# Which queue issues the conditioning loads of a hybrid decoder layer: GpSimd's or SyncE's, from the output gate's stage on

## The chip, the cores and the metric

The kernel runs on one NeuronCore of a Trainium2 chip. That core has five engines with instruction streams of their own: TensorE (PE, matrix products), VectorE (DVE), ScalarE (ACT), GpSimd (POOL) and SyncE (SP, which computes nothing and issues transfers). Sixteen DMA engines move data between main memory and the on-chip memory. A transfer is issued by an instruction in the stream of SP, ACT or POOL; in the profile the transfers of SP stand as queue q1, those of POOL as q0, and those of ACT as q10. An engine works through its instructions in order, so an instruction that waits for a semaphore holds up everything behind it on that engine.

The metric is the device time of one launch in microseconds. The kernel before takes 1963.89 us (median of 3 runs, 1963.37 to 1964.3).

## What is computed

One inference step of one layer (`DEPTH = 1`), in float32, for 256 prompt tokens and 8 x 4 sample tokens together: N = 288 columns, model width 2048.

```python
mod = silu(c) @ w_ada + b_ada                       # 2048 -> 6 x 2048
sh1, sc1, gt1, sh2, sc2, gt2 = split(mod, 6)
xn = rmsnorm(x, g_norm1) * (1 + sc1) + sh1
proj = xn @ w_in
...
merged = (gate0 * (y_lru @ w_br_lru) + gate1 * (y_gla @ w_br_gla)
          + gate2 * (y_ml @ w_br_ml))               # y_ml = sigmoid(m_o) * rmsnorm(h)
x = x + gt1 * (merged @ w_out)
xn = rmsnorm(x, g_norm2) * (1 + sc2) + sh2
x = x + gt2 * (square(relu(xn @ w_ff1)) @ w_ff2)
y = rmsnorm(x, g_final)
```

The conditioning product is the first line: `w_ada` is a 2048 x 12288 matrix (six pieces of 2048 columns), multiplied by only nine vectors (one for the prompt, eight for the samples). Its results are needed at different times: sc1 and sh1 at the start, gt1 when the output projection ends, sh2 and sc2 for the second norm, gt2 at the very end. The three recurrent branches (RG-LRU, GLA, mLSTM) also read and update states; the one that matters here is the mLSTM's matrix memory of the samples (`state_mlstm_C`, read as 16 tiles `mC`, written as `o_C_s`).

## The kernel before

**The weight stream.** All large products go through `stream` (line 148). It walks a weight block in groups of 256 rows x 512 columns (one tile of 128 x 1024, 512 KB). For each group SP loads `raw` (line 155), ACT makes the rounded `hi` (line 156), DVE makes the rest `lo` (line 158), and PE runs 24 matmuls (line 165: four column blocks, two row blocks, and the products hi x xh, hi x xl, lo x xh). `raw`, `hi` and `lo` have three buffers each. `run` (line 191) drives a stream: after each group it takes one step of the pattern in `pace` and one step of each generator in `side` (the recurrent branches, which run between the groups).

**The conditioning product.** `units` (line 344) yields its pieces: 64 units of 1 MB for GT1, SH2, SC2 and GT2 (16 each), after the smaller ones for SC1 and SH1. A unit has a load (`ada`, line 302; the transfer is line 308, or line 306 twice where the tile is in two halves) and a product (`products`, matmuls on line 269). `load_one` (line 356) issues the next unit's load, `visit` (line 361) runs the products of all units held. A pattern set by `every` is a string of steps, one for each group: `L` loads one unit, `V` visits, `.` does nothing; `skip` leaves out that many groups first. `slots["ids"]` says which buffers the units take in turn: `None` is the tile `ag`, `"st"` the two tiles `st`, a number one of the ten slots `s0` to `s9`, `"xh"` and `"xl"` halves of the tiles that held the activations. `slots["queue"]` says which engine issues the load.

**The queues.** SP's order is written out by hand: `manual_schedule` (line 68) keeps its instructions in the order in which the program emits them. The orders of the other engines come from a planner that places instructions by priority and expected time, so that POOL may issue a load well before the place where the program emits it. The first conditioning loads go through SP (line 235); line 588, ahead of the stage of the remaining value columns, sets the queue to POOL, and nothing sets it again. POOL issues the `mC` loads of the mLSTM too (line 1396); ACT issues its stores (line 1437).

**The stages around the change**, in program order:

- `merge(1)` (line 1512) ends; its last gate tile is in `ag` (line 1085), its last activations are in slots 8 and 3.
- The output gate's stage, lines 1513 to 1523: two blocks of eight groups. Units go to `ag` and slot 8. The pattern loads after the 12th and the 13th of the 16 groups and visits after the 15th. The mLSTM runs beside it: every three groups a pair of `mC` tiles is used (`inter`, line 1412), updated and stored, in two `st` tiles or two halves of slot 9 by turns.
- `merge(2)`, from line 1524: 48 groups, units in `ag`, `st`, slot 5. From the seventh group on, in rounds of seven: three loads after three successive groups, a visit after the next, then three groups without a step. Six rounds, 18 units.
- The output projection, from line 1530: 32 groups. Loads after groups 7 to 12 (six in succession), a visit after the 14th, then eight more loads after groups 16, 17, 19, 20, 22, 23, 25, 26, which are visited at the end of the stage, beside the second norm. 14 units.
- The feed-forward part, from line 1633: the last six units, after groups 1, 4 and 7 of rounds of 20 groups with the visit after the 13th, from the second hidden block on.

That is 2 + 18 + 14 + 6 = 40 units from line 1513 on. Ten of them go to `st` and take two transfers, so there are 50 transfers.

Of the kernel before, what the change touches and what calls it, by code (L numbers as in the profile page):

```python
# [52 lines left out]
def trunk(ctx, tc, io):  # L53
    nc = tc.nc
    PSUM = bass.MemoryType.PSUM
    V, S, G, T, Q = nc.vector, nc.scalar, nc.gpsimd, nc.tensor, nc.sync
# [130 lines left out]
    def every(p, skip=0):  # L187

        pace.update(every=p.split(), n=-skip)
# [45 lines left out]
    slots = {"ids": (None,), "n": 1, "queue": Q}  # L235
# [1274 lines left out]
    ml_ = beside(mlstm())  # L1510

    merge(1, ygla, io["wbg"])
    slots.update(ids=(None, 8), n=0)
    every("L L . V" + 12 * " .", skip=11)

    mo = slot(3)
# [255 lines left out]
```

## Time and profile before

| what | before |
|---|---|
| median of 3 runs | 1963.89 us |
| profiled execution, its own time | 1962.52 us |
| its span, first to last instruction | 1960.7 us |
| PE busy | 1921.1 us (98%) |
| DVE / ACT / POOL busy | 1028.6 / 823.7 / 267.2 us |
| main memory read / written | 409.85 / 16.81 MB |
| mean granted TensorE clock | 0.995 |

The profiled execution's time is 1.8 us above its span: what lies ahead of the first and behind the last instruction. The median of the runs is 1.37 us above the profiled execution. Times inside the trace count from the span's start. A name such as `st<-wada` is a transfer into the tile `st` from the tensor `wada`; `PE pi L1412` is a matmul on line 1412 that writes the tile `pi`. A row of the view of waits tells who waited for whom, the total, how many times and the longest. A row of the view by stretch gives the busy time of PE, weight loads, DVE, ACT and POOL with their numbers of instructions, then the granted clock, the DMA engines' busy share and GB/s.

### The profile page before, as it was taken

To read this page: it belongs to the slowest core of one execution; us is meant where nothing else is said; L and a number is where in the kernel's file an instruction comes from. 1 tells how busy PE (TensorE), PEld (TensorE's weight loads), DVE (VectorE), ACT (ScalarE), POOL (GpSimd) and SP (SyncE) were. 2 spreads that over 40 slices of the span, in tenths; PEclk is the share of its full clock that TensorE was granted. 3 is DMA by queue.
4 is the path that set the end of the run, shared out by engine and by line. 5 is a ranking of instruction groups with operands and counts; after the bars stand their busy time and mean duration, and the time that the engine had idled before them with its cause. 6 is when DMAs were issued, how large, how long until landed. Compare 5 with 4: busy or idle time off the path is not lost.

```text
span 1960.7 us, 35959 instructions
## 1 busy us (share of the span) xinstructions
PE 1921.1 (98%) x15060; PEld 1819.7 (93%) x15060; DVE 1028.6 (52%) x1567; ACT 823.7 (42%) x1179; POOL 267.2 (14%) x373
## 2 busy tenths in 40 slices
PE   7999999999999998999999999999999999999997
PEld 4889889999899997899998899999999999999997
DVE  2574746545683456654445564445444445444565
ACT  3433374544454343443333453443333334343433
POOL 0011200000132000012224431000000000010101
PEclk9999999999999999999999999999999999999999
DMA  9998766547744368957797555444444444444442
GB/s 385 408 381 301 262 243 239 199 151 262 267 149 145 136 205 296 310 215 272 276 360 280 190 187 204 169 159 169 169 163 160 172 162 162 162 168 170 164 172 106
DMA packets 116338, 429.01 MB, mean 219 GB/s; under 512 B 11776, under 2 KB 12064, under 8 KB 116048
## 3 DMA queue, kind: packets, MB, share of 16 engines
q1 hardware_dynamic: 85888, 313.26, 44.1%
q0 software_dynamic: 25536, 96.27, 13.4%
q10 hardware_dynamic: 4752, 17.19, 2.2%
q8 instruction: 118, 1.93, 0.4%
q14 instruction: 44, 0.36, 0.1%
HBM read 409.85 MB, written 16.81 MB: 218 GB/s over the span
## 4 chain that ended last, share of the span: by engine, by line
PE 93%; DMA 4%; DVE 2%; ACT 1%; issue 0%; DVEq 0%; SPq 0%; ACTq 0%; POOLq 0%
PE mm L165 83%; PE pa L269 4%; DMA raw<-win 2%; DMA st<-mC 1%; DMA raw<-wout 1%; DVE lo L158 1%; DMA s<-wada 0%; ACT hi L156 0%; PE px L677 0%; PE px L1429 0%; PE pi L1412 0%; PE px L948 0%; PE px L1343 0%; DVE s L597 0%; DMA o_C_s<-st 0%
## 5 line engine op out<-in xcount | busy, mean ns | idle before, releaser
L158 DVE TENSOR_TENSOR lo<-raw,hi 128x1024 fp32r<-128x1024 f32 x448 | 552.0, 1233 | 591.6 <-ACT hi L156 577.0
L156 ACT ACTIVATE hi<-raw 128x1024 fp32r<-128x1024 f32 x448 | 473.9, 1060 | 797.2 <-PE mm L165 656.8
L165 PE MATMUL mm<-xh,hi 128*128 128x288 f32 x2560 | 757.1, 300 | 2.9 <-ACT xh L493 1.8
L165 PE MATMUL mm<-xl,hi 128*128 128x288 f32 x2560 | 753.4, 297 | 0.0
L165 PE MATMUL mm<-xh,lo 128*128 128x288 f32 x2560 | 737.3, 296 | 1.6 <-DVE lo L158 1.6
L165 PE MATMUL mm<-s,hi 128*128 128x288 f32 x3328 | 659.5, 296 | 0.8 <-DVE rs_t L1545 0.8
L165 PEld LDWEIGHTS mm<-s,hi 128*128 128x128 f32 x3328 | 529.3, 188 | 6.3 <-issue 5.8
L165 PEld LDWEIGHTS mm<-xh,hi 128*128 128x128 f32 x2560 | 479.8, 188 | 21.8 <-issue 12.3
L165 PEld LDWEIGHTS mm<-xl,hi 128*128 128x128 f32 x2560 | 481.9, 188 | 2.7 <-issue 1.3
L165 PEld LDWEIGHTS mm<-xh,lo 128*128 128x128 f32 x2560 | 476.0, 188 | 4.2 <-DVE lo L158 2.7
L165 PE MATMUL mm<-s,lo 128*128 128x288 f32 x1664 | 477.3, 295 | 0.6 <-DVE lo L158 0.6
L165 PEld LDWEIGHTS mm<-s,lo 128*128 128x128 f32 x1664 | 308.6, 188 | 2.0 <-DVE lo L158 1.0
L158 DVE TENSOR_TENSOR lo<-s,hi 128x1024 fp32r<-128x1024 f32 x80 | 98.0, 1225 | 115.2 <-ACT hi L156 115.2
L1607 POOL TENSOR_TENSOR t<-t 128x288 f32<-128x288 f32 x64 | 60.2, 952 | 625.7 <-ACT t L1606 625.7
L156 ACT ACTIVATE hi<-s 128x1024 fp32r<-128x1024 f32 x80 | 84.9, 1061 | 143.2 <-PE mm L165 142.6
L1623 DVE TENSOR_TENSOR s<-s,mm 128x288 f32<-128x288 f32 x96 | 40.3, 450 | 33.9 <-PE mm L165 32.7
L269 PE MATMUL pa<-s,silc 128*32 128x256 f32 (+1 forms) x616 | 49.8, 450 | 5.5 <-DMA s<-wada 5.5
L269 PEld LDWEIGHTS pa<-s,silc 128*32 128x32 f32 x616 | 18.9, 112 | 25.5 <-issue 11.1
L429 DVE TENSOR_TENSOR s<-t,s 128x288 fp32r<-128x288 f32 x64 | 33.8, 568 | 15.5 <-ACT s L428 15.5
L308 POOL DMA_DIRECT2D ag<-wada x23 | 16.5, 719 | 169.7 <-PE pa L269 169.5
L428 ACT ACTIVATE s<-t 128x288 fp32r<-128x288 f32 x64 | 28.1, 443 | 24.6 <-POOL t L1607 24.6
L395 POOL TENSOR_TENSOR row<-row,t 128x288 f32<-128x288 f32 x24 | 22.4, 934 | 116.1 <-ACT t L393 115.1
(403 smaller groups left out, 1117.8 us busy)
## 6 DMA issues: line engine op xcount, KB each, us to landing
raw<-win SPq DMA_DIRECT2D x192, 512.0 KB, 4.4
raw<-wf SPq DMA_DIRECT2D x176, 512.0 KB, 4.1
s<-wf SPq DMA_DIRECT2D x80, 512.0 KB, 3.2
s<-wada SPq DMA_DIRECT2D x28, 1024.0 KB, 9.2
ag<-wada POOLq DMA_DIRECT2D x23, 1024.0 KB, 7.2
s<-wada POOLq DMA_DIRECT2D x21, 1024.0 KB, 10.9
raw<-wout SPq DMA_DIRECT2D x32, 512.0 KB, 4.7
st<-wada POOLq DMA_DIRECT2D x28, 512.0 KB, 8.0
```

The costliest lines, as they stand in the source:

```text
L156: pace["hi"] = S.activation(hi, raw, AF.Copy)
L158: pace["lo"] = V.tensor_tensor(out=lo, in0=raw, in1=hi.bitcast(F32), op=ALU.subtract)
L165: pace["last"] = T.matmul(ps, w[:, kk, ms], x, start=k == k0 and i == 0, stop=k == kt - 1 and i == 2)
L269: pace["prod"] = T.matmul(ps[32 * j:32 * j + 32, h * w // 4:(h + 1) * w // 4], stat(k), v[:, j], start=k == 0 and h == 0, stop=k == KT - 1 ...
L308: slots["queue"].dma_start(raw[0].rearrange("p (h m) -> p h m", h=2), wada[kind, :, k].rearrange("h p m -> p h m"))
L395: G.tensor_tensor(out=s, in0=s, in1=sq, op=ALU.add)
L428: S.activation(dst_h[:, r], src[:, r], AF.Copy)
L429: V.tensor_tensor(out=dst_l[:, r], in0=src[:, r], in1=dst_h[:, r].bitcast(F32), op=ALU.subtract)
L1607: G.tensor_tensor(out=r, in0=r, in1=r, op=ALU.mult)
L1623: V.tensor_tensor(out=a, in0=a, in1=p, op=ALU.add)
```

## The change

One line: where the output gate's stage sets the buffers of its units, it also sets the queue back to SyncE's. Since nothing sets the queue later, this holds for all 40 units from there to the end. Their loads keep their place in the program, their buffers and their visits. Because SP's order is the program's order, each load now stands on SP between the weight load of the group after which the pattern has its `L` and the weight load of the next group; on POOL they are gone.

```diff
@@ -1510,7 +1510,7 @@
     ml_ = beside(mlstm())
 
     merge(1, ygla, io["wbg"])
-    slots.update(ids=(None, 8), n=0)
+    slots.update(ids=(None, 8), n=0, queue=Q)
     every("L L . V" + 12 * " .", skip=11)
 
     mo = slot(3)
```

## The prediction

> **What bounds the kernel now.** I began with the page's head and its table of queues, then asked for PE's waits in the part of the span that the change touches.
>
> ```profile
> span 1960.7 us, 35959 instructions
> PE 1921.1 (98%) x15060; PEld 1819.7 (93%) x15060; DVE 1028.6 (52%) x1567; ACT 823.7 (42%) x1179; POOL 267.2 (14%) x373
> ...
> q1 hardware_dynamic: 85888, 313.26, 44.1%
> q0 software_dynamic: 25536, 96.27, 13.4%
> ```
>
> PE is busy 98% of the span: a change of queues can only win back idle PE time, or add some. The waits of PE between 755 and 1290 us, from the first moved load to the last visit, are three:
>
> ```profile
> PE pi L1412 <- DMA st<-mC: 7.6, 1, 7.6
> PE mm L165 <- DVE rs_t L1545: 0.8, 1, 0.8
> PE mm L165 <- DVE lo L158: 0.6, 1, 0.6
> ```
>
> The large one is a state tile of the mLSTM that came late. POOL's timeline shows what was issued around it, PE's timeline the gap, and the chain of waits the transfer itself:
>
> ```profile
> 755.39 0.53 POOL L1396 DMA_DIRECT2D st<-mC  x1 [7.83 <-DVE s L1110]
> 755.91 0.71 POOL L308 DMA_DIRECT2D s<-wada  x1
> 756.62 0.72 POOL L308 DMA_DIRECT2D ag<-wada  x1
> 758.37 0.56 POOL L1396 DMA_DIRECT2D st<-mC  x1 [1.03 <-DMA o_C_s<-st]
> ...
> 767.16 0.29 PE L165 MATMUL mm<-xl,hi 128*128 128x288 f32 x1
> 775.07 1.08 PE L1412 MATMUL pi<-st,s 128*32 128x257 f32 x8 [7.62 <-DMA st<-mC]
> ...
> 758.37 16.66 DMA st<-mC
> ```
>
> Two conditioning loads of 1 MB went into POOL's queue at 755.91 and 756.62, and the second `mC` load of the pair, issued behind them, took 16.66 us. These two are exactly the units of the output gate's stage: the planner had issued them as soon as their buffers were free. The transfers issued between 755 and 776 us, by queue (kind, size, median us to landing), show that those in POOL's queue came last:
>
> ```profile
> raw<-win SPq DMA_DIRECT2D x3, 512.0 KB, 10.4
> o_C_s<-s ACTq DMA_DIRECT2D x2, 514.0 KB, 8.8
> ag<-wada POOLq DMA_DIRECT2D x1, 1024.0 KB, 16.8
> ```
>
> By stretch (columns as told above):
>
> ```profile
> 767.00:772.00 5.00, 0.45 (x4) 0.21 (x2) 0.90 (x3) 2.77 (x6) 0.54 (x1) 1.00 1.02 418
> 772.00:775.00 3.00, 0.00 (x0) 0.00 (x0) 0.00 (x0) 0.00 (x0) 0.53 (x1) 0.50 1.03 404
> 775.00:779.00 4.00, 3.93 (x21) 3.12 (x22) 2.44 (x6) 0.00 (x0) 0.00 (x0) 0.52 0.17 68
> 779.00:800.00 21.00, 21.00 (x166) 19.87 (x166) 12.25 (x23) 8.80 (x14) 1.58 (x3) 1.00 0.86 280
> 1006.00:1031.00 25.00, 23.68 (x176) 23.07 (x174) 11.25 (x13) 8.79 (x10) 0.36 (x1) 1.00 0.96 387
> ```
>
> The DMA engines were full during the wait (418 and 404 GB/s), and the idle PE lost its clock: it worked from 775 to 779 us at 0.52. The last row is the other weak place, the start of the output projection, where PE is idle for 25.00 - 23.68 = 1.3 us.
>
> **The change part by part.** *The two loads of the output gate's stage leave POOL's queue.* The `mC` load at 758.37 then has nothing between it and the pair's first. What such loads take otherwise (least, median, most, first those from 690 to 756 us, then from 765 to 806):
>
> ```profile
> DMA to landing us min/median/max: 4.5/6.1/7.7
> DMA to landing us min/median/max: 4.0/6.0/7.7
> ```
>
> At the most, 7.7 us, it lands at 766.1, ahead of PE's arrival at about 767.45 (the start of PE's last matmul, and its length). So I take the whole wait: -7.6 us, with bounds 0 (it lands as late as now) and -7.6. The clock goes with it: (1 - 0.52) x 4 us = -1.9 us, bounds 0 and -1.9. The Trainium skill (TensorE: Matmul & The Clock Gate, "What's actually happening") puts the half clock after one idle window of about 3.4 us; the trace agrees, with 7.6 us idle and 0.50 from 772 on, and by that rule a rest of the wait under 3 us would cost no clock.
>
> *Where the two loads go.* On SP they stand behind the 12th and 13th weight loads of the stage:
>
> ```profile
> 790.50 8.41 SPq L155 DMA_DIRECT2D raw<-win  x3
> ...
> 824.65 1.85 PE pa L269 x16
> ```
>
> These three weight loads are the 12th to 14th (the gate's 16 begin 11 loads earlier, at the end of merge 1's), so the loads move from 756 to some 35 us later, 9.5 us less when PE is ahead by that. Their visit is at 824.65, so they are not late. But there they meet `mC` loads and stores of the next pairs: the stretch from 779 to 800 moved 280 GB/s x 21 us = 5.9 MB, and with 2.1 MB more it is 8.0 MB, 380 GB/s, against 404 to 418 in the full stretches. It fits, barely. I set +0.5 us, with bounds 0 and +5.1 (the 2.1 MB at 415 GB/s, all of it falling on one late `mC` tile).
>
> *What stands behind a 1 MB load on SP.* A weight load is not needed at once. The groups, from the chain of waits, and the makers of `hi` and `lo`, from the page:
>
> ```profile
> 863.68 2.72 PE pa L269 x32
> 866.39 22.58 PE mm L165 x168
> ...
> L158 DVE TENSOR_TENSOR lo<-raw,hi 128x1024 fp32r<-128x1024 f32 x448 | 552.0, 1233 | 591.6 <-ACT hi L156 577.0
> L156 ACT ACTIVATE hi<-raw 128x1024 fp32r<-128x1024 f32 x448 | 473.9, 1060 | 797.2 <-PE mm L165 656.8
> ...
> L155 SPq DMA_DIRECT2D raw<-win x20: 327/328/328, 864.3 to 961.3; - x20
> ...
> DMA to landing us min/median/max: 3.1/4.2/8.2
> ```
>
> 168 matmuls are seven groups, so a group is 3.22 us; ACT waits for PE, not for data, 656.8 us in all. With three buffers each, `raw` of group g can be loaded when `lo` of g-3 is made, that is when PE has ended g-6 plus the split of 1.06 + 1.23 = 2.3 us; PE wants it split when it ends g-1. From issue to need that leaves 5 x 3.22 - 2 x 2.3 = 11.5 us, of which the landing takes 4.2 (the median; 3.1 at least, so 1.9 us beside the 1.26 us that 0.52 MB takes at 415 GB/s).
>
> *Merge 2* is the tightest, since SP must wait there: the load into `ag` stands four groups behind the visit that frees it, and SP runs five to six groups ahead of PE. The visit of 863.68 ends at 866.4; only then does SP issue three units and, between and behind them, three weight loads, 3 x 1.05 + 3 x 0.52 = 4.7 MB. At 415 GB/s the last weight tile lands 11.3 + 1.9 = 13.2 us later; it is needed after six groups less the split, 19.3 - 2.3 = 17.0 us. Margin 3.8 us, cost 0. That SP's queue alone reaches such a rate is in the stretch from 0 to 30 us, slow start included (all queues, then q1 with its packets, MB and share):
>
> ```profile
> DMA packets 3088, 11.45 MB, mean 382 GB/s; under 512 B 223, under 2 KB 351, under 8 KB 3087
> q1 hardware_dynamic: 2719, 9.97, 82.7%
> ```
>
> *The output projection* has six loads in succession: per group 1.57 MB, 3.8 us at 415 GB/s against 3.22, a backlog of 6 x 0.6 = 3.4 us, under the 11.5 - 3.2 = 8.3 us left. Before, eight units were asked for at once there, ahead of the weights, at 387 GB/s; spread out and in order they should give back some of the idle 1.3 us. I take -1.0, bounds -1.3 and +3 (about the backlog, uncovered).
>
> *Issuing.* SP gets 50 issues of 0.328 us, 16 us, covered by its waits for buffers. POOL loses these:
>
> ```profile
> L308 POOL DMA_DIRECT2D s<-wada x13: 703/706/775, 755.9 to 1215.7; - x13
> L308 POOL DMA_DIRECT2D ag<-wada x11: 703/721/772, 756.6 to 1216.5; - x11
> ...
> L306 POOL DMA_DIRECT2D st<-wada x20: 528/544/561, 811.1 to 1217.8; - x20
> ```
>
> With six into `xh` and `xl`, 30 x 0.71 + 20 x 0.54 = 32 us. PE's waits above name no POOL work, so both are 0. In the feed-forward part the loads are three groups apart with visits six groups later: 0.
>
> **Sum:** -7.6 - 1.9 - 1.0 + 0.5 = -10.0 us against the profiled execution's 1962.5 (span 1960.7), so 1952.5; the median of the runs lies 1.4 above it: 1953.9 us.
>
> **The rivals.** *Bytes, not queues.* The stall could come from full DMA engines rather than from the order inside POOL's queue; then it only moves to a later `mC` pair. For it: 404 to 418 GB/s during the wait, and 380 expected after 779. Against it: in the same 20 us the stores took 8.8 and the weights 10.4, the `mC` load 16.66, and the stretch after it needs 380 only if nothing spreads. Price: 5.1 us of wait and most of the clock's and the projection's gain, some 9 us given back: 1963. The Trainium skill (DMA: Bandwidth & Descriptors, "Issuing engines are not separate DMA queues") says that all issuers share the same engines and that only issue time is saved, which alone gives this outcome. Its section "Queues, rings and completion order" has each engine take turns between the queues, which speaks for the order inside one queue; the 16.66 beside 8.8 agrees with that.
>
> *SP's queue starves the weights*, the slower side. Weight loads that had a queue of their own stand behind 1 MB loads and behind SP's wait for `ag`. It decides by the rate SP's queue gets. At 290 GB/s merge 2 needs 16.2 + 1.9 against 17.0, 1.1 us in each of five rounds; the projection's backlog is 6 x 2.2 = 13.2 against 11.5 - 3.7 = 7.8, 5.4 more: 11 us, the gain is gone. At 270 it is 5 x 2.3 + 8 = 19.5 us: 1973. For it: SP does wait, and margins are 3 to 5 us. Against it: the 382 GB/s above.
>
> *Half.* The `mC` load still takes as long as the weights did, 10.4 us, and lands at 768.8, 1.4 us late, and the later pairs lose 3 us more: +4, 1958.
>
> **How the numbers follow.** Forecast 0.68, with its own range from 1951 (all bounds on the good side but for noise) to 1957.5 (3 to 4 us of contention); bytes 0.13; starved 0.13; half 0.06. A measurement of this kernel tells 0.2%, 3.9 us, from no change. Faster: 0.68 + 0.06 = 0.74; same 0.13; slower 0.13. The range from 1950.5 to 1965 takes in the forecast, the half and the first rival, and leaves out most of the starved case.
>
> **What would show it.** Right: in the changed profile PE's wait for `st<-mC` is gone, the clock stays 1.00 near 770 us, `mC` loads land within 8 us or so, and PE works without new waits in merge 2. Wrong: an `mC` wait at a later pair (bytes); waits of PE for `lo` or of ACT for `raw` after each visit of merge 2 or in the projection (starved); or a planner's new order that puts something else in front of PE, which the rows before cannot show.

## The result, and the profile after

| | before | after |
|---|---|---|
| median of the runs | 1963.63 us (4 runs, 1961.43 to 1964.3) | 1949.83 us (4 runs, 1949.48 to 1950.38) |
| ratio after / before | | 0.9932, 95% interval 0.9915 to 0.9949 |
| span of the profiled execution | 1960.7 us | 1947.9 us |
| mean granted clock | 0.995 | 0.998 |

The kernel is 13.8 us faster by the medians, 12.8 us by the spans. The forecast was 1953.9 us with a range from 1950.5: the direction and the main cause were right, the gain was 3.8 us more than the 10.0 of the forecast, and the time is just under the range.

The list of PE's waits between 740 and 1290 us is empty in the changed profile: the three waits shown before are all gone. Where the time went is seen best when the same group's first matmul is looked up in both traces (us from the span's start; the groups are those of the weight stream):

```
group                          before     after     after - before
output gate, 3rd               762.39     762.26     -0.1
output gate, 5th               780.41     770.59     -9.8
merge 2, 1st                   830.44     819.93    -10.5
output projection, 7th        1021.84    1011.17    -10.7
output projection, 13th       1042.94    1030.31    -12.6
stream, end of last matmul     1945.56    1932.89    -12.7
```

Nearly all of it falls in two places: 9.7 us at the late `mC` tile, 2.0 us at the start of the output projection; 0.9 us lie in smaller steps between. POOL's timeline after has no conditioning load among the `mC` loads, and SP's has them between the weights:

```profile
753.97 0.53 POOL L1396 DMA_DIRECT2D st<-mC  x1 [7.32 <-PE mm L165]
758.24 0.53 POOL L1396 DMA_DIRECT2D st<-mC  x1 [3.74 <-DMA o_C_s<-st]
...
779.90 0.33 SPq L155 DMA_DIRECT2D raw<-win  x1
780.58 0.38 SPq L308 DMA_DIRECT2D ag<-wada  x1
785.85 0.33 SPq L155 DMA_DIRECT2D raw<-win  x1
786.28 0.38 SPq L308 DMA_DIRECT2D s<-wada  x1
```

The second `mC` load was issued at 758.24, as before at 758.37, and landed in 6.5 us. All 16 `mC` loads now land within 9.6 us, where one took 16.66 before; the 9.6 is that of the load at 781.26, beside the two conditioning loads on SP, and a little over the 8 us or so that the prediction named as the sign of being right (least, median, most):

```profile
DMA to landing us min/median/max: 3.6/6.1/9.6
```

By stretch, the rows that answer to those shown of before; the last is the stretch of 1006 to 1031 us of before, moved by the 10.6 us that PE is ahead:

```profile
767.00:772.00 5.00, 5.00 (x39) 5.00 (x40) 3.97 (x11) 2.95 (x7) 0.53 (x1) 1.00 0.99 311
772.00:775.00 3.00, 3.00 (x25) 3.00 (x24) 2.59 (x5) 0.64 (x1) 0.00 (x0) 1.00 0.90 304
775.00:779.00 4.00, 4.00 (x39) 3.25 (x38) 1.57 (x2) 3.40 (x7) 0.53 (x1) 1.00 0.98 307
779.00:800.00 21.00, 21.00 (x185) 20.36 (x184) 13.97 (x33) 7.44 (x12) 1.59 (x3) 1.00 0.99 377
995.40:1020.40 25.00, 25.00 (x190) 25.00 (x189) 13.20 (x22) 9.23 (x12) 2.06 (x3) 1.00 0.96 365
```

PE is busy throughout and its clock stays at 1.00. The stretch from 779 to 800 us moves 377 GB/s, against the 380 worked out in the prediction, and no work of PE comes late in it. The last row is where the prediction's arithmetic failed: 190 matmuls in 25 us against 176 before, 14 more at 0.134 us each (22.58 us for 168), which is 1.9 us, although the busy column differs by only 1.3 us. (Both traces hold all 24 matmuls of all 528 groups, so none of the 14 is a missing record.)

### The profile page after: what moved, and what is told of

Its sections match the earlier page's. It is cut to its first block, busy times and chain, and to the rows that moved or that the text cites. A ratio compares the mean times of both kernels' runs of the same rounds, so it can differ in the third digit from the quotient of the medians.

```text
span 1947.9 us, 35935 instructions
## 1 busy us (share of the span) xinstructions
PE 1917.1 (98%) x15060; PEld 1816.6 (93%) x15060; DVE 1030.4 (53%) x1567; ACT 824.0 (42%) x1179; POOL 235.9 (12%) x323
## 4 chain that ended last, share of the span: by engine, by line
PE 96%; DVE 1%; DMA 1%; ACT 1%; issue 0%; DVEq 0%; SPq 0%; ACTq 0%
PE mm L165 85%; PE pa L269 5%; DMA raw<-win 1%; PE px L1429 0%; DMA s<-wada 0%; PE px L677 0%; PE pi L1412 0%; DVE lo L158 0%; ACT hi L156 0%; PE px L948 0%; PE px L1343 0%; DVE s L597 0%; PE px L1353 0%; PE pi L966 0%; PE px L1015 0%
## 5 line engine op out<-in xcount | busy, mean ns | idle before, releaser
L1110 POOL TENSOR_TENSOR s<-s,t 128x288 f32<-128x288 f32 x16 | 20.0, 1274 | 179.0 <-DVE t L1109 179.0
```

What stands on the lines that cost most here:

```text
L1110: (V if br == 1 else G).tensor_tensor(out=a, in0=a, in1=t, op=ALU.add)
```

## The experiments

Each is a whole kernel, run beside the kernel before on the same chip. The kernel before had medians of 1962.89, 1962.77 and 1962.83 us in the three groups of runs, and each ratio is to the kernel before of the same group. Edits are shown against the changed kernel. "By the starts of PE's groups" means the difference between two traces in the start of the same weight group's first matmul.

**Which loads carry the gain: the gate's two alone.**

```diff
-    slots.update(ids=(None, "st", 5), n=0)
+    slots.update(ids=(None, "st", 5), n=0, queue=G)
```

> Only the two loads of the output gate's stage go through SP; the 38 from merge 2 on go through POOL as before. If the gain is the late mC tile and its half clock, 9.7 us of the 12.8 us of the changed profile are here, and the start of the output projection loses its 2.2 us again (start to start of PE's groups): about 1952 us, with no PE wait for st<-mC. If the gain came mainly from the 38 other loads, it stays above 1958.

Measured: 1952.31 us (1951.89 to 1953.2), ratio 0.9947 (0.9932 to 0.9961). No wait for `st<-mC`, clock 1.00. PE's waits in the trace are two at the projection, as before (0.8 and 0.5 us), and one of 0.7 us for an `mC` tile ahead of the output gate's stage. Two of the 40 loads carry 10.6 us.

**The other half: the 38 later loads alone.**

```diff
-    slots.update(ids=(None, 8), n=0, queue=Q)
+    slots.update(ids=(None, 8), n=0)
...
-    slots.update(ids=(None, "st", 5), n=0)
+    slots.update(ids=(None, "st", 5), n=0, queue=Q)
```

> The opposite half: the two loads of the output gate's stage stay on POOL, the 38 others go through SP. Theory of the late mC tile: the wait of about 7.6 us and a stretch of half clock near 772 us are there again, the projection's 2.2 us are won: about 1960.5 us. Rival (the other 38 loads carry the gain): under 1954.

Measured: 1962.08 us (1959.21 to 1963.78), ratio 0.9995 (0.9985 to 1.0004). Of PE's waits from 740 to 1290 us only this is left:

```profile
PE pi L1412 <- DMA st<-mC: 6.1, 1, 6.1
```

The half clock is there for 6.8 us again. The projection's 2.0 us are won in the trace (its 13th group comes 2.0 us earlier against its 7th), but the medians differ by only 0.8 us, and the expected time was 1960.5. The late tile itself is not the same from one execution to the next: in the three profiled ones that have it at this place (before, this kernel and a later one) it lands in 16.66, 15.39 and 15.11 us and PE waits 7.6, 6.1 and 6.7. That this hides the projection's gain in the medians is likely, not shown.

**Order in the queue, or bytes: the same bytes at the same time, through SP.** The two loads stand after the 4th and 5th group; their visit stays.

```diff
-    every("L L . V" + 12 * " .", skip=11)
+    every("L L" + 9 * " ." + " V" + 12 * " .", skip=3)
```

> All 40 loads on SP, but the two of the output gate's stage stand after its 4th and 5th group, so that SP issues them when ag comes free, near 755 us, just when POOL issued them before; their visit stays after the 15th group. The same bytes in the same 20 us, in another queue. If the order inside POOL's queue made the mC tile late: the tile lands within 10 us of its issue, PE waits 1 us at most there, 1950 to 1952 us. If full DMA engines made it late, whatever the queue: mC lands after 14 us or more, PE waits 5 us or more and loses the clock, 1956 to 1960 us.

Measured: 1954.06 us (1953.32 to 1954.53), ratio 0.9956 (0.9939 to 0.9972). SP issues the loads at the time when POOL issued them before:

```profile
754.91 0.38 SPq L308 DMA_DIRECT2D ag<-wada  x1
755.38 0.42 SPq L155 DMA_DIRECT2D raw<-win  x1
755.91 0.43 SPq L308 DMA_DIRECT2D s<-wada  x1
```

The `mC` load issued at 757.48 lands in 10.1 us, not 16.7, the clock stays up, and PE waits 1.6 us for a later `mC` tile. The fair pair for it is the kernel just above, which also has the 38 others on SP and differs by the queue of the two early loads: 1962.08 against 1954.06, 8.0 us. So most of the loss was the order inside POOL's queue. Asking for the loads 25 us earlier still costs 4 us against the changed kernel, 2 more than expected. The chain of waits has a weight load behind the first of them and the later `mC` tile:

```profile
755.38 10.98 DMA raw<-win
...
786.24 9.13 DMA st<-mC
```

How much of the 4 us is full DMA engines, and how much weights that now stand behind 1 MB loads on SP, is not told apart.

**The loads on POOL, held back.** A first attempt asked the planner to put each load behind the `hi` of its group:

```diff
-    slots.update(ids=(None, 8), n=0, queue=Q)
+    slots.update(ids=(None, 8), n=0, queue=G, placed=True)
...
-            held.append((u[0], u[1](), u[2], u[3]))
+            with tc.issue_after(pace["hi"].ins) if slots.get("placed") else nullcontext():
+                held.append((u[0], u[1](), u[2], u[3]))
```

> All 40 loads stay on POOL, but the planner may not put them ahead of the hi of the group after which the program has them, so that they are issued about when SP would. If it is the time of issue (the planner's 35 us ahead of the program) and not the queue that costs: no wait of 5 us or more for mC, 1950 to 1954 us. If POOL's queue is the trouble at any time: an mC tile of a later pair comes late behind the two loads and PE waits again 5 us or more, 1957 to 1964 us.

Measured: 1962.09 us (1959.99 to 1964.32), ratio 0.9994 (0.9985 to 1.0003). It tells nothing of either theory, since the loads did not move: placed behind an instruction of ACT, they still went out on POOL near 755 us (one added line moves 1396 to 1397).

```profile
754.66 0.53 POOL L1397 DMA_DIRECT2D st<-mC  x1 [7.62 <-DVE t L1110]
755.18 0.71 POOL L308 DMA_DIRECT2D s<-wada  x1
755.88 0.72 POOL L308 DMA_DIRECT2D ag<-wada  x1
759.24 0.56 POOL L1397 DMA_DIRECT2D st<-mC  x1 [2.63 <-DMA o_C_s<-st]
```

Placed behind an instruction of POOL itself, they do move. The next two kernels put the gate's two loads on POOL behind a chosen `mC` load, and keep the 38 others on SP (added lines move 1396 to 1400 and 1412 to 1416):

```diff
+    mc_load = {}
...
-            G.dma_start(tiles[n], io["mC"][n])
+            mc_load[n] = G.dma_start(tiles[n], io["mC"][n])
...
-    slots.update(ids=(None, 8), n=0, queue=Q)
+    slots.update(ids=(None, 8), n=0, queue=G, behind=12)
...
-    slots.update(ids=(None, "st", 5), n=0)
+    slots.update(ids=(None, "st", 5), n=0, queue=Q, behind=None)
...
-            held.append((u[0], u[1](), u[2], u[3]))
+            b = slots.get("behind")
+            with tc.issue_after(mc_load[b].ins) if b is not None else nullcontext():
+                held.append((u[0], u[1](), u[2], u[3]))
```

> The two loads of the output gate's stage go through POOL, placed right behind the mC load of tile 12 and so ahead of those of tiles 13, 14 and 15, near 778 us, about when SP issues them in the changed kernel; the other 38 stay on SP. If it is the order inside POOL's queue: the load of tile 13 takes 13 us or more, PE waits 4 to 6 us for it about 795 us, 1954 to 1958 us. If only the time of issue counted (the early issue beside a fuller stage): no new mC wait over 1 us, 1949 to 1951 us as with SP.

Measured: 1958.72 us (1956.35 to 1959.9), ratio 0.998 (0.997 to 0.9989). POOL's timeline, the chain of waits and PE's wait show the old picture two pairs later:

```profile
777.05 0.53 POOL L1400 DMA_DIRECT2D st<-mC  x1 [6.27 <-DVE lo L158]
777.57 0.71 POOL L308 DMA_DIRECT2D ag<-wada  x1
778.27 0.72 POOL L308 DMA_DIRECT2D s<-wada  x1
780.65 0.56 POOL L1400 DMA_DIRECT2D st<-mC  x1 [1.66 <-DMA o_C_s<-st]
...
780.65 16.66 DMA st<-mC
...
PE pi L1416 <- DMA st<-mC: 5.5, 1, 5.5
...
799.00:802.00 3.00, 3.00 (x14) 3.00 (x14) 2.04 (x6) 0.00 (x0) 0.00 (x0) 0.50 0.33 129
```

The load behind the two takes 16.66 us again, PE waits 5.5 us, and then works at 0.50 of its clock. The two loads go out 3 and 8 us earlier than in the changed kernel (777.57 and 778.27 against 780.58 and 786.28), in which the same `mC` load, issued at 781.26, took 9.6 us with them on SP. The time is 0.7 us above the expected range.

> As before on POOL, but behind the last mC load (tile 15), near 797 us; the other 38 on SP. Order inside POOL's queue: nothing stands behind the two loads, so no wait, 1949 to 1951 us: POOL's queue is as good as SP's. If POOL's queue as such were the trouble: 1953 or more.

With `behind=15`: 1951.26 us (1950.24 to 1952.12), ratio 0.9941 (0.9925 to 0.9958). The loads go out on POOL at 795.86 and 796.57, nothing that PE awaits stands behind them, and the largest `mC` wait is 0.4 us. POOL's queue as such is not the trouble. The medians lie 1.4 us above the changed kernel's, and 0.3 above the expected range. The spans differ by 1.7 us: 0.5 us is already there at the gate's first group, 0.3 come between there and merge 2, and 0.9 behind the last weight group. I leave that difference open.

**Whether SP's wait can starve the weights.** The visit of merge 2 stands two groups later, so the next load into `ag` follows it by two groups.

```diff
-    every("L L L V . . .", skip=6)
+    every("L L L . . V .", skip=6)
```

> Changed kernel, but in merge 2 the visit stands two groups later, so that the next load into ag stands two groups behind the visit that frees it instead of four. Theory that SP's wait holds up the weights behind it: by the margin of 3.8 us less two groups of 3.22 us, weights come 2.6 us late in each of five rounds: 8 to 18 us more, 1958 to 1968 us, with waits of PE for lo after each visit. Rival (SP's wait is covered by the three buffers anyway): within 2 us of 1949.8.

Measured: 1961.49 us (1960.09 to 1964.48), ratio 0.9995 (0.9986 to 1.0004), 11.7 us above the changed kernel. SP's waits and PE's, in merge 2:

```profile
SPq L308 <- PE pa L269: 46.8, 5, 11.0
...
PE mm L165 <- ACT hi L156: 7.5, 9, 1.3
```

SP waits for the visit before the load into `ag`, five times, and PE then waits for `hi` (`lo` was expected), made from weights that stood behind. By the starts of PE's groups merge 2 is 13.1 us longer than in the changed kernel: 2.6 on average in each of five rounds, as worked out.

> The same late visit in merge 2, with the loads from merge 2 on through POOL (the gate's two on SP), so that the wait for ag holds up POOL and not the weights. Same theory: about as the kernel with only the gate's two loads on SP, 1951 to 1954 us. Rival (the late visit itself costs, whatever the queue): as much slower as its twin on SP.

The same late visit with the loads on POOL (`queue=G` from merge 2 on): 1952.14 us (1952.1 to 1954.74), ratio 0.995 (0.9935 to 0.9965). PE waits nowhere in merge 2. A late visit costs nothing when the wait for its buffer stands on POOL; 2.2 us are lost at the projection, as in the kernel with only the gate's loads on SP.

**The margin at the projection.** Eight loads behind four groups:

```diff
-    every("L L L L L L . V ." + " L L ." * 4 + 20 * " .", skip=6)
+    every("LL LL LL LL . . . V ." + " L L ." * 3 + 20 * " .", skip=6)
```

> Changed kernel, but the output projection loads eight units behind four groups, two behind each, where it loaded six behind six; the visit after the 14th group stays, six more units follow. Per group 2.62 MB, 6.3 us at 415 GB/s against 3.2: a backlog of four times 3.1 us, against some 4 us that lo is ahead of PE when the loads begin: weights 8 us late, PE waits 6 to 10 us, 1956 to 1960 us. If SP's queue did not starve the weights (margin of 8 us as predicted): 1950 to 1954 us.

Measured: 1964.94 us (1963.12 to 1968.46), ratio 1.0013 (1.0004 to 1.0023). PE's waits and SP's in that stage:

```profile
PE mm L165 <- ACT hi L156: 7.4, 4, 2.8
...
SPq L308 <- PE pa L269: 18.7, 1, 18.7
```

By the starts of PE's groups the burst costs 7.3 us, as expected. Another 6.1 us are lost at a second place that the expectation missed: with eight loads ahead, the next two go into halves of `xh` two groups behind the visit that frees them, and SP waits 18.7 us there with the weights behind it. PE's clock fell to half twice, for 3.4 us each. A further 1.2 us were lost in the gate's stage, which this edit leaves as it is, with a wait of 1.0 us for an `mC` tile.

**All conditioning loads through SP.**

```diff
-    slots.update(ids=(5, 6, 7, None, 0, 3), n=0, queue=G)
+    slots.update(ids=(5, 6, 7, None, 0, 3), n=0)
```

> All conditioning loads through SP: also those from the stage of the remaining value columns up to the gate's stage, 13 + 3 of the shift product and the units of merge 0 and 1 among them. PE waits nowhere in that stretch on POOL's loads, so the theory (only a late tile that PE waits for counts) says no change: 1948.5 to 1951.5 us, unless a load waits on SP for its buffer and holds up weights, which would show as waits of PE for lo between 140 and 740 us. Rival (SP's queue is the better one everywhere): 1947 us or less.

Measured: 1954.97 us (1952.78 to 1956.57), ratio 0.9959 (0.9944 to 0.9974): 5 us worse than the changed kernel. Between 140 and 760 us SP now waits for visits:

```profile
SPq L308 <- PE pa L269: 63.7, 12, 11.7
SPq L320 <- PE pa L269: 21.4, 5, 7.1
...
PE mm L165 <- DVE s L1106: 1.9, 1, 1.9
PE mm L165 <- DVE lo L158: 1.4, 2, 0.7
PE mm L165 <- ACT hi L156: 1.0, 1, 1.0
```

PE's waits there are small singly, but its groups fall behind by 3.5 us between 215 and 252 us, and by 1.0 and 1.6 us near 339 and 492 us. SP's queue is not the better one everywhere. That it is so where the pattern leaves enough groups between a visit and the next load into its buffer fits these waits and those of merge 2, but was not varied in this stretch. None of these kernels beats the changed one.

## Why the prediction was right, and where it failed

**The step that failed** is the sizing of three smaller terms of the sum, not its mechanism. The collision was put at +0.5 us with a bound of 0 on the good side, and -0.7 came; the output projection was put at -1.0 with a bound of -1.3, and -2.0 came; the 1.4 us added for the distance between the median and the profiled execution were 0.1 after the change. With every bound on its good side the sum is 1962.5 - 10.8 = 1951.7 us for the profiled execution; it was 1949.74.

**The late `mC` tile: right.** Forecast -7.6 us of wait and -1.9 us of clock, -9.5; by the starts of PE's groups it is -9.7. That the order inside POOL's queue made it late is shown from three sides: the same bytes at the same time through SP give 10.1 us of landing and no loss of clock; the two loads on POOL ahead of a later tile bring the wait and the half clock back there; behind the last tile they cost no wait. The view of transfers from 755 to 776 us of before has the other of the two loads too, and that from 763 to 771, when all three queues had work, what each queue moved (packets, MB, share):

```profile
s<-wada POOLq DMA_DIRECT2D x1, 1024.0 KB, 11.8
...
q0 software_dynamic: 312, 1.20, 36.7%
q1 hardware_dynamic: 297, 1.09, 33.4%
q10 hardware_dynamic: 279, 1.04, 32.0%
```

POOL's queue landed its transfers in the order of their issue: `s` at 767.7, `ag` at 773.4, `mC` at 775.0. It moved 1.20 MB in 8 us beside the other two queues, so that 2.1 MB take some 14 us (an estimate from these rows), and the tile stood behind them. The rival of bytes has at most a smaller share: loading early through SP costs 4 us.

The Trainium skill (DMA: Bandwidth & Descriptors, "Issuing engines are not separate DMA queues") says that issuing from several engines saves issue time alone. Here the measurement decides against it: 8.0 us lie between the two early loads on SP and on POOL. By the Trainium skill's section "Queues, rings and completion order" on the same page, each engine takes turns between the queues it has work for. The three nearly equal rows agree with that, as do the stores of ACT's queue that landed in 8.4 and 9.3 us beside POOL's 16.66 in the run with the loads ahead of tile 13.

One remark of the prediction on the clock does not hold: that a rest of the wait under 3 us would cost none. In the kernel with the doubled loads waits of 2.51 and 2.78 us were enough (the rows stand in the last section).

**The collision of the two loads at their new place: right in its traffic, wrong in its price.** 377 GB/s came, 380 were worked out, but the +0.5 us was not paid. From the 5th gate group to merge 2 PE gained another 0.7 us; the kernel with only the gate's loads moved has it too, the one with only the 38 others moved has not, so it goes with these two loads. What it is made of stays open: the planner also put PE's own instructions in another order there, which no run separates.

**The output projection: a bound that was none.** The prediction took -1.0 us with a bound of -1.3, because the idle time of the stretch was 25.00 - 23.68. It was -2.0. A matmul counts as busy for some 0.30 us but the next one starts 0.13 us after its start, so the first 0.17 us of every stall do not show as idle. The rows of before show it:

```profile
1028.09 0.29 PE L165 MATMUL mm<-s,lo 128*128 128x288 f32 x1
1029.15 0.50 PE L165 MATMUL mm<-s,hi 128*128 128x288 f32 x2 [0.76 <-DVE rs_t L1545]
```

From start to start it is 1.06 us, 0.93 more than the usual 0.13; the wait says 0.76. Counted by matmuls, 176 against 190, the stretch had 1.9 us to give. The chain of waits of before leads into the second stall of this stretch over weight loads:

```profile
1010.21 9.43 DMA raw<-wout
...
1022.09 6.48 DMA raw<-wout
...
1031.05 18.45 PE mm L165 x136
```

Such a load takes 4.7 us in the median. These two stood in SP's queue, so it was not the order inside POOL's queue that made them late. That it was the eight loads asked for at once is made likely by this and by the doubled loads, which cost 7.3 us on SP; a spread pattern on POOL was not tried.

**The median against the profile.** The sum was made against 1962.5 us and 1.4 us were added, since the three runs then shown lay so far above the profiled execution. That was chance for the most part: in 19 later runs the kernel before has 1962.89, 0.4 above the profiled execution, and after the change the profiled execution (1949.74) lies within 0.1 us of the median. Of the 4.1 us between forecast and result this term carried 1.3, the collision 1.2, the projection 1.0 and the late tile 0.2; the remaining 0.4 lies in small steps all along the span.

**The starved weights: rightly called unlikely, but the margin was counted too large.** Merge 2's arithmetic held: 2.6 us a round were worked out for a visit two groups later, and 2.6 came on average. At the projection the prediction left 8.3 us less 3.4 of backlog, 4.9 us. In the changed trace `lo` of the 13th group is the first of the two in the row below: it starts at 1028.3, takes 1.2 us and ends at 1029.5. Its group starts on PE at 1030.3, so 0.8 us were left.

```profile
L158 DVE TENSOR_TENSOR lo<-raw,hi x2: 1226/1226/1226, 1028.3 to 1029.5; 128x1024 fp32r<-128x1024 f32 x2
...
ACT hi L156 <- DMA raw<-wout: 13.0, 6, 2.9
```

A tile that lands late also makes its `hi` and `lo` late (ACT waited for weights six times, as it had before the change), and the next load into that buffer is issued late in turn: SP issued the 13th group's weights at 1018.7, when `lo` of the 10th had just ended. The prediction counted every load as issued on time.

## What to carry to other kernels

A load that has long to go and a load that an engine will soon wait for should not share a queue in that order: here the second landed only after the first, however little the first was needed. Moving the patient loads into a queue with a hand-written order is safe only as long as that queue's waits for their buffers are shorter than the lead of what stands behind. In the changed kernel SP waited 30.9 us for visits between 760 and 1290 us, six times and 8.2 us at most, and PE never noticed. Count the groups between the visit and the next load: with four it cost nothing in merge 2 and with two it cost 2.6 us a round. When pipelined matmuls are bounded, count starts, not idle time.

## What was not expected of the hardware

**The clock falls after less than 3 us of waiting.** In the kernel with the doubled loads at the projection, PE's rows after its two longest waits, and the stretches around the first:

```profile
1031.01 2.08 PE L165 MATMUL mm<-s,hi 128*128 128x288 f32 x8 [2.51 <-ACT hi L156]
1062.26 2.29 PE L165 MATMUL mm<-s,hi 128*128 128x288 f32 x8 [2.78 <-ACT hi L156]
...
1027.86:1031.27 3.41, 0.90 (x7) 0.66 (x7) 0.28 (x1) 1.18 (x2) 0.00 (x0) 1.00 0.94 383
1031.27:1034.69 3.42, 3.42 (x16) 3.42 (x16) 3.38 (x3) 2.00 (x2) 0.00 (x0) 0.50 0.45 133
```

In the 3.41 us ahead of the half clock PE had worked for 0.90 us, so a stretch need not be idle throughout. The wait of 1.6 us for an `mC` tile in the kernel with the early loads through SP cost no clock.

**Kernels in which PE waits for transfers scatter.** Before: 1961.32 to 1966.63 us in 19 runs; the 38 later loads alone: 4.6 us from least to most in ten runs; the tile moved to the later pair: 3.6 in ten. Late weights go with as much: 4.4 and 5.3 us in ten runs of the late visit and of the doubled loads on SP, 3.8 in four runs with all loads on SP. The changed kernel has 0.9, only the gate's loads on SP 1.3, the early loads through SP 1.2 (four runs each, and fewer runs show less of a scatter). That the waited-for transfer is what varies is likely, not shown.
